# Gate weights split a job earlier, the SSD state update one step later, and plain transposes in the mLSTM turn

## The chip, the cores and the metric

The kernel runs on one core of a Trainium2 chip. A core has five engines with queues of their own: TensorE (PE) multiplies matrices and transposes, VectorE (DVE), ScalarE (ACT) and GpSimd (POOL) do elementwise work, SyncE (SP) issues nearly all DMAs here. The metric is the device time of one execution in microseconds (us). Before the change three runs took 1884.36, 1888.11 and 1892.07 us; the median is 1888.11.

## The reference

A decoder layer with two parallel groups of heads over a sequence of 2048 tokens of width 1024, all in float32:

```python
h = rms_norm(x, norm_w)
proj = h @ w_in                       # 1024 x 6680
q, k, v, i, f, o, z_m, z_s, xbc, dt = split(proj)
# four mLSTM heads, chunks of 128 tokens: matrix memory C, normaliser n
hm = mlstm_chunkwise(q, k, v, log_i, log_f)
hm = hm * rsqrt(mean(hm * hm) + EPS) * w * sigmoid(o) * silu(z_m)
# two SSD groups of eight heads, chunks of 128: state h
xs, B, C = split(silu(causal_conv(xbc)))
y = ssd_chunked(xs, dt, A, B, C) + d_skip * xs
y = y * silu(z_s); y = y * rsqrt(mean over group(y * y) + EPS) * w
x = x + concat(hm, y) @ w_out
return rms_norm(x, final_norm_w)
```

In `ssd_chunked` a chunk gives `y_diag` (from its own tokens), `y_off` (from the state that the chunks before left), and then `h = decay * h + B^T (weights * x)`. In the mLSTM a chunk's rows are divided by a norm per row before they are gated.

## The kernel before, in words

The projections are large matrix products in two stages (the two halves of the sequence, 1024 tokens each) and two more stages for the output projection (one per half of the mixed columns). Each product of a pair of column blocks is a Strassen-like form of seven products; each has twelve matmuls of 128x128 by 128x512 (four slices of the inner size; high times high, high times low, low times high of a float32r split). A *job* is one such pair: 26 in each of the stages 0 and 1, 8 in each of the stages 2 and 3. `strassen` (L273) yields after each product, and the main loop (L1031) interleaves job n with the first two products of job n + 1.

The right operands (`R11`, `R21`, `T2`, `T3`, `T1`, `R22`, `T4`, high and low, 1 MB each) stay in SBUF for a whole stage. In the last job of a stage each is refilled from DRAM after its last use (`refill`, L387). Those of stage 1 are made ahead of time by `next_h` (L493), which runs in the background from the end of phase h1 on: for each of four chunks it loads two blocks of tokens into `xt` (the one buffer `t`, which the convolution's `cd` and the gates' `tz` use too), normalises them (`tok_norm`), turns them on PE (`tok_turn`, L414) some calls later, and writes seven sums out, each split into `hqh` and `hql` (three buffers `hq`, L395) and stored. The line `at(3 + i * 82 // total, bgq)` spreads its calls over the steps. `next_w` (L520) does the same with the output weights in stage 1.

A *step* is one product: `step` (L1002) prepares left operands (`left`), refills, runs what is due (`tick`, `later`), what is planned (`at`), and pulls the recurrence of the phase before along (`Weave.to`). The order of PE's instructions is the order in which the program writes them; the other engines' order is chosen by the scheduler of the framework, near the program's order. Every engine works its queue in order.

The gate columns of the projection have matmuls of their own, `gates_mm` (L541): four small loads of weights into `wg`, two DVE operations that make two sums, a split into `wgs`, then 24 matmuls with R11 and R21 and 24 with R22 and T3. For stage 1 its head is called at the head of job 26, the first of that stage, and the matmuls follow at the first and the third step.

`rec_head` (L665) does one mLSTM head: `scores`, `memory`, and four steps later `turn` (L743), where PE multiplies the rows `mx` by a diagonal matrix `dgm` (identity times the row's factor, made on POOL), which turns and scales them at once. `rec_group` (L776) does one SSD group. A chunk goes through `decay` (loads `E`, subtracts on DVE, exponential on ACT), `tokens` (DVE makes `xdt`, `cbm`, `xw` and then `E` times `cbm`), `states` (PE: the old state's part L842, then the new state L852), a step later `outs` (PE L870), and `norm` and `spread` three and five steps after that. `E` has a single buffer.

Of the kernel before, what the change touches and what calls it, by code (L numbers as in the profile page):

```python
# [10 lines left out]
F32R = mybir.dt.float32r  # L11
# [6 lines left out]
P = 128  # L18
# [51 lines left out]
def hybrid_layer(ctx, tc, x, norm_w, w_in, b_igate, b_fgate, conv_w, conv_b, dt_bias,  # L70
# [422 lines left out]
    def next_h():  # L493

        for c in range(NCH):
# [3 lines left out]
            for i in range(2):  # L499
# [4 lines left out]
                tok_norm(SUP + i * TB + c * P, None, xt)  # L504
                for _ in range(4):
                    yield
# [34 lines left out]
    def gates_mm(s, R):  # L541
        wg = r2("wg", 4 * 4 * NG)
        wv = wg.rearrange("p (o k c) -> p o k c", o=4, k=4)
# [5 lines left out]
        nc.vector.tensor_scalar_mul(wv[:, 3], wv[:, 0], -1.0)  # L549
        wh = mk([P, 1024], "t", 1, "wgs", F32R) if s else mk([P, 6, P], "g3", 2, "wgs", F32R).rearrange("p a b -> p (a b)")  # L550
        hi, lo = wh[:, 0:16 * NG], wh[:, 16 * NG:32 * NG]
        nc.scalar.copy(hi, wg)
# [112 lines left out]
    def rec_head(s, h):  # L665
# [38 lines left out]
        def memory(n):  # L704
# [26 lines left out]
            nc.gpsimd.tensor_tensor(sq, sq, mhalf, op=ALU.pow)  # L731
            dg = r5("dgm")
            nc.gpsimd.tensor_scalar_mul(dg, ident, sq)
            L["m", n] = (mx, dg)

# [7 lines left out]
        def turn(n):  # L743
            b, c = seq[n]
            mx, dg = L.pop(("m", n))
            g = L.pop(("gt", n))
            ps = rc_tile()
            for i in range(2):
                nc.tensor.matmul(ps[:, i * P:(i + 1) * P], lhsT=mx[:, i * P:(i + 1) * P], rhs=dg,
                                 start=True, stop=True)  # L750
            nc.vector.tensor_mul(g, ps[:, 0:2 * P].rearrange("p (a l) -> p a l", a=2), g)
            nc.sync.dma_start(mixd[0][b * NCH + c][:, 2 * h:2 * h + 2, :], g)
# [23 lines left out]
    def rec_group(s, g):  # L776
# [30 lines left out]
        def tokens(n):  # L807
# [7 lines left out]
            for i in range(4):  # L815
                nc.tensor.transpose(xps[:, i * P:(i + 1) * P], t[:, 2 + i, :], ident)
            xdt = r2("xdt")
            nc.vector.tensor_tensor(xdt.rearrange(v3, e=HD), xps.rearrange(v3, e=HD),
                                    bc(G["sp"][:, c, ws], HD), op=ALU.mult)
            bt = r5("bt")  # L820
            nc.scalar.copy(bt, cps[:, P:2 * P])
            cbm = r5("cbm")
            nc.vector.tensor_mul(cbm, cps[:, 0:P], tri)
            xw = r2("xw")
            nc.vector.tensor_tensor(xw.rearrange(v3, e=HD), xps.rearrange(v3, e=HD),
                                    bc(G["dend"][:, c, hs], HD), op=ALU.mult)
            E = L["E", n][0]
# [3 lines left out]
        def states(n):  # L831
# [5 lines left out]
            H = S.get("H")  # L837
            y = r2("y").rearrange("p (a l) -> p a l", a=4)
            if H is not None:
                ops = rc_tile()  # L840
                for i in range(4):
                    nc.tensor.matmul(ops[:, i * P:(i + 1) * P], lhsT=H[:, i * P:(i + 1) * P],  # L842
                                     rhs=t[:, 1, :], start=True, stop=True)
                nc.vector.tensor_mul(y, ops.rearrange("p (a l) -> p a l", a=4), ea)
                for i in range(4):
                    nc.scalar.activation(ea[:, i, :], t[:, 2 + i, :], AF.Copy, scale=dcol[:, g, i:i + 1])
                nc.vector.tensor_add(y, y, ea)
            else:
                for i in range(4):
                    nc.scalar.activation(y[:, i, :], t[:, 2 + i, :], AF.Copy, scale=dcol[:, g, i:i + 1])  # L850
            sps = rc_tile()
            nc.tensor.matmul(sps, lhsT=bt, rhs=xw, start=True, stop=True)  # L852
            if H is None:
                H = S["H"] = mk([P, GW], "H", 1, "H")
                nc.vector.tensor_copy(H, sps)
            else:
                nc.gpsimd.tensor_tensor(H.rearrange(v3, e=HD), H.rearrange(v3, e=HD),
                                        bc(G["cdec"][:, c, hs], HD), op=ALU.mult)
                nc.vector.tensor_add(H, H, sps)
            L["y", n] = y  # L860

        def outs(n):
# [14 lines left out]
            nc.vector.tensor_mul(y, y, z)  # L877
            nc.scalar.activation(z, y, AF.Square)
            nc.gpsimd.tensor_add(z[:, 0:2, :], z[:, 0:2, :], z[:, 2:4, :])
# [33 lines left out]
        for n in range(len(seq)):  # L913
            states(n)
            if s == 0 and n + 1 == len(seq):
                nc.sync.dma_start(hdd[g], S["H"])
            yield
            outs(n)
# [112 lines left out]
    for n, jb in enumerate(jobs):  # L1031
        g = jb["gen"]
        if jb["new"] and "s" in jb:
            s = jb["s"]
            gm = gates_mm(s, Rs[s]) if s else gm0
            if s:
                next(gm)
                at(1, gm)
# [34 lines left out]
        if "s" in jb and (n + 1 == len(jobs) or jobs[n + 1].get("ph") != jb["ph"]):  # L1073
            nxt = [k for k in jobs[n + 1:] if k.get("ph") == jobs[n + 1].get("ph") and k["stage"] == jobs[n + 1]["stage"]]
            wv.set(rec(jb["s"], jb["ph"]), NREC[jb["ph"][0]], 7 * len(nxt) if "s" in jobs[n + 1] else 42)
            if jb["ph"] == "h1":
                bgq = next_w() if jb["s"] else next_h()
                total = 64 if jb["s"] else 68
                for i in range(total):
                    at(3 + i * 82 // total, bgq)  # L1080
        if jb["stage"] == 2 and n + 1 < len(jobs) and jobs[n + 1]["stage"] == 3:
# [29 lines left out]
```

## Time and profile before

| what | before |
|---|---|
| median of three runs | 1888.11 us |
| profiled execution | 1880.11 us, span 1878.4 us |
| PE, PE weight loads busy | 1693.1 us (90%), 1380.0 us (73%) |
| DVE, ACT, POOL busy | 1299.4 us (69%), 899.9 us (48%), 398.6 us (21%) |
| DMA | 405.33 MB, mean 216 GB/s |
| mean granted PE clock | 0.960 of full speed |

The span runs from the first to the last instruction. Busy time of an engine is the union of its instructions. PE's matmuls overlap one another, so a group's busy time is not its cost; the distance between starts is nearer to that. The idle time that stands behind a group is that of its engine just before it, with what ended it.

### The profile page before, as it was taken

The page shows a single profiled execution, that of the slowest core. Times are in us where ns is not written, and L with a number is a line of the kernel's source. Part 1 is how long each engine was busy: PE and PEld are TensorE (multiplying, and loading weights), DVE is VectorE, ACT ScalarE, POOL GpSimd, SP SyncE. Part 2 cuts the span into 40 slices and gives each one's busy share as a digit, 9 for nine tenths or more (in the row PEclk, how much of TensorE's full clock was granted, in tenths as well). Part 3 has the DMA queues.
Part 4 walks back from the last instruction along what each step waited for, and adds up shares of the span by engine and source line. Part 5 has one row for each costly group of instructions (what it writes and reads, how often), then busy time and mean ns, then how long its engine had stood idle before and what let it go on. Part 6 is the DMA issues. An engine that isn't in the chain of part 4 may idle for free.

```text
span 1878.4 us, 25378 instructions
## 1 busy us (share of the span) xinstructions
PE 1693.1 (90%) x8200; PEld 1380.0 (73%) x8200; DVE 1299.4 (69%) x2417; ACT 899.9 (48%) x1912; POOL 398.6 (21%) x597
## 2 busy tenths in 40 slices
PE   5999999899999793998999999989979878997997
PEld 4688887788788681776788878768768667776885
DVE  7677968966657782697685886565668557863775
ACT  5345644465566551343554455555556433432443
POOL 2000303223121220032121231201112134431322
PEclk8999999999999896998999999999989989998999
DMA  5355667578778699364565758888867977578553
GB/s 149 96 166 171 192 197 214 176 244 249 233 210 233 185 308 358 98 198 134 181 181 162 240 176 271 257 285 274 270 195 256 358 264 223 185 254 336 181 161 112
DMA packets 358323, 405.33 MB, mean 216 GB/s; under 512 B 30224, under 2 KB 284432, under 8 KB 352816
## 3 DMA queue, kind: packets, MB, share of 16 engines
q1 hardware_dynamic: 358192, 403.72, 66.7%
q8 instruction: 65, 1.06, 0.2%
q14 instruction: 66, 0.54, 0.1%
HBM read 251.40 MB, written 152.24 MB: 215 GB/s over the span
## 4 chain that ended last, share of the span: by engine, by line
PE 32%; DMA 22%; DVE 12%; issue 5%; ACT 4%; SPq 3%; POOL 2%; DVEq 0%; POOLq 0%; ACTq 0%
PE pj L270 26%; DMA E<-arow 4%; DMA nmi<-mrow 3%; DVE E L797 2%; DMA we<-in_w_out 2%; DVE cd L317 2%; DMA wb<-in_w_in 1%; DMA xr<-in_x 1%; PE rc L852 1%; DMA T4l<-ws1T 1%; DMA mx<-mix 1%; DVE hql L398 1%; DMA z<-gd 1%; PE rc L870 1%; DMA ws1T<-hqh 1%
## 5 line engine op out<-in xcount | busy, mean ns | idle before, releaser
L730 POOL TENSOR_SCALAR sq<-dn,sq 128x1 f32<-128x1 f32 x64 | 50.3, 785 | 663.0 <-ACT sj L728 532.2
L270 PE MATMUL pj<-R22h,S4h 128*128 128x512 f32 x272 | 118.3, 435 | 34.7 <-ACT ob L289 19.1
L270 PE MATMUL pj<-T2h,S2h 128*128 128x512 f32 x272 | 114.9, 423 | 2.3 <-ACT T2h L441 2.3
L270 PE MATMUL pj<-T1l,S1h 128*128 128x512 f32 x272 | 107.9, 397 | 8.8 <-DMA T1l<-ws1T 7.0
L270 PE MATMUL pj<-T1h,S1h 128*128 128x512 f32 x272 | 113.1, 416 | 2.5 <-ACT ob L283 2.4
L270 PE MATMUL pj<-T4h,L22h 128*128 128x512 f32 x272 | 113.3, 416 | 1.9 <-DMA T4h<-ws1T 1.9
L270 PE MATMUL pj<-R11h,L11h 128*128 128x512 f32 x272 | 113.9, 419 | 0.0
L270 PE MATMUL pj<-R21h,L12h 128*128 128x512 f32 x272 | 112.9, 415 | 0.0
L270 PE MATMUL pj<-R22l,S4h 128*128 128x512 f32 x272 | 111.6, 410 | 0.0
L270 PE MATMUL pj<-R22h,S4l 128*128 128x512 f32 x272 | 111.6, 410 | 0.0
L270 PE MATMUL pj<-T2l,S2h 128*128 128x512 f32 x272 | 108.2, 398 | 3.2 <-DMA T2l<-ws0T 1.9
L270 PE MATMUL pj<-T3h,S3h 128*128 128x512 f32 x272 | 109.7, 403 | 0.0
L270 PE MATMUL pj<-T4l,L22h 128*128 128x512 f32 x272 | 106.9, 393 | 1.9 <-DMA T4l<-ws1T 1.9
L270 PE MATMUL pj<-T2h,S2l 128*128 128x512 f32 x272 | 108.0, 397 | 0.0
L270 PE MATMUL pj<-T1h,S1l 128*128 128x512 f32 x272 | 107.6, 396 | 0.0
L270 PE MATMUL pj<-T4h,L22l 128*128 128x512 f32 x272 | 106.9, 393 | 0.0
L270 PE MATMUL pj<-R21l,L12h 128*128 128x512 f32 x272 | 106.5, 392 | 0.0
L270 PE MATMUL pj<-R21h,L12l 128*128 128x512 f32 x272 | 106.5, 391 | 0.0
L270 PE MATMUL pj<-R11h,L11l 128*128 128x512 f32 x272 | 106.3, 391 | 0.0
L270 PE MATMUL pj<-T3l,S3h 128*128 128x512 f32 x272 | 106.1, 390 | 0.2 <-DMA T3l<-ws0T 0.2
L270 PE MATMUL pj<-T3h,S3l 128*128 128x512 f32 x272 | 106.1, 390 | 0.0
L270 PE MATMUL pj<-R11l,L11h 128*128 128x512 f32 x272 | 106.1, 390 | 0.0
(331 smaller groups left out, 4681.4 us busy)
## 6 DMA issues: line engine op xcount, KB each, us to landing
wa<-in_w_in SPq DMA_DIRECT2D x52, 512.0 KB, 5.3
s<-sum SPq DMA_DIRECT2D x52, 512.0 KB, 5.5
hd<-ob SPq DMA_DIRECT2D x32, 512.0 KB, 4.2
E<-arow SPq DMA_DIRECT2D x32, 512.0 KB, 5.4
hin<-hd SPq DMA_DIRECT2D x64, 256.0 KB, 5.6
mx<-mix SPq DMA_DIRECT2D x32, 512.0 KB, 4.4
wb<-in_w_in SPq DMA_DIRECT2D x26, 512.0 KB, 4.8
sum<-ls SPq DMA_DIRECT2D x26, 512.0 KB, 3.8
```

What stands on the lines that cost most here:

```text
L270: nc.tensor.matmul(ps, lhsT=l[:, k, :], rhs=r[:, k, :], start=start and k + n == 0, stop=k == 3 and n == 2, skip_group_check=True)
L317: nc.vector.scalar_tensor_tensor(dst, raw[:, q:q + SUP], cw[:, t, q:q + 1], dst, op0=ALU.mult, op1=ALU.add)
L398: nc.vector.tensor_sub(lo, src, hi.bitcast(F32))
L730: nc.gpsimd.tensor_scalar(sq, dn, DV * EPS, sq, op0=ALU.mult, op1=ALU.add)
L797: nc.vector.tensor_scalar(E[:, r, :], E[:, r, :], G["cum"][:, c, k:k + 1], 0.0, op0=ALU.subtract, op1=ALU.min)
L852: nc.tensor.matmul(sps, lhsT=bt, rhs=xw, start=True, stop=True)
L870: nc.tensor.matmul(yps[o:o + HD, (r // 2) * P:(r // 2 + 1) * P], lhsT=xdt[:, r * HD:(r + 1) * HD], rhs=E[:, r, :], start=True, stop=True, ...
```

## The change

Five things are changed. The head of `gates_mm` for stage 1 is called at the head of job 25, one job earlier, and its three tiles are taken from the `hq` buffers. In `rec_group` the matmul L852 and the addition to H move from `states` into a new `update`, which is called a step later, ahead of `outs`; `xw` and `bt` are made first in `tokens`; the D term is written into `y` by ACT ahead of the old state's part, which is multiplied into `ea` and added; the decay of H on POOL stays in `states`. The square in `outs` moves from ACT to POOL. In `rec_head` POOL scales `mx` in place, and `turn` transposes it. `next_h` yields six times instead of four between a load and its turn, with 84 calls over 76 steps instead of 68 over 82.

```diff
@@ next_h
-                for _ in range(4):
+                for _ in range(6):
                     yield
@@ gates_mm
-        wg = r2("wg", 4 * 4 * NG)
+        wg = mk([P, 512], "hq", 3, "wg")[:, 0:16 * NG] if s else r2("wg", 4 * 4 * NG)
...
-        wh = mk([P, 1024], "t", 1, "wgs", F32R) if s else mk([P, 6, P], "g3", 2, "wgs", F32R).rearrange("p a b -> p (a b)")
-        hi, lo = wh[:, 0:16 * NG], wh[:, 16 * NG:32 * NG]
+        if s:
+            hi, lo = (mk([P, 512], "hq", 3, "wgs", F32R)[:, 0:16 * NG] for _ in range(2))
+        else:
+            wh = mk([P, 6, P], "g3", 2, "wgs", F32R).rearrange("p a b -> p (a b)")
+            hi, lo = wh[:, 0:16 * NG], wh[:, 16 * NG:32 * NG]
@@ rec_head, memory and turn
-            dg = r5("dgm")
-            nc.gpsimd.tensor_scalar_mul(dg, ident, sq)
-            L["m", n] = (mx, dg)
+            nc.gpsimd.tensor_scalar_mul(mx, mx, sq)
+            L["m", n] = mx
...
-                nc.tensor.matmul(ps[:, i * P:(i + 1) * P], lhsT=mx[:, i * P:(i + 1) * P], rhs=dg,
-                                 start=True, stop=True)
+                nc.tensor.transpose(ps[:, i * P:(i + 1) * P], mx[:, i * P:(i + 1) * P], ident)
@@ rec_group, tokens: order now bt, xw, xdt, cbm, E times cbm
+            bt = r5("bt")
+            nc.scalar.copy(bt, cps[:, P:2 * P])
+            xw = r2("xw")
+            nc.vector.tensor_tensor(xw.rearrange(v3, e=HD), xps.rearrange(v3, e=HD),
+                                    bc(G["dend"][:, c, hs], HD), op=ALU.mult)
             xdt = r2("xdt")
...
@@ rec_group, states, update and outs
+            for i in range(4):
+                nc.scalar.activation(y[:, i, :], t[:, 2 + i, :], AF.Copy, scale=dcol[:, g, i:i + 1])
             if H is not None:
...
-                nc.vector.tensor_mul(y, ops.rearrange("p (a l) -> p a l", a=4), ea)
-                for i in range(4):
-                    nc.scalar.activation(ea[:, i, :], t[:, 2 + i, :], AF.Copy, scale=dcol[:, g, i:i + 1])
+                nc.vector.tensor_mul(ea, ops.rearrange("p (a l) -> p a l", a=4), ea)
                 nc.vector.tensor_add(y, y, ea)
...
+                nc.gpsimd.tensor_tensor(H.rearrange(v3, e=HD), H.rearrange(v3, e=HD),
+                                        bc(G["cdec"][:, c, hs], HD), op=ALU.mult)
+            L["y", n] = y
+
+        def update(n):
+            bt, xdt, xw = L["a", n]
+            H = S.get("H")
             sps = rc_tile()
             nc.tensor.matmul(sps, lhsT=bt, rhs=xw, start=True, stop=True)
...
-            nc.scalar.activation(z, y, AF.Square)
+            nc.gpsimd.tensor_mul(z, y, y)
...
             states(n)
+            yield
+            update(n)
             if s == 0 and n + 1 == len(seq):
                 nc.sync.dma_start(hdd[g], S["H"])
-            yield
             outs(n)
@@ main loop
+        if n + 1 < len(jobs) and jobs[n + 1]["new"] and "s" in jobs[n + 1]:
+            S["gm"] = gates_mm(jobs[n + 1]["s"], Rs[jobs[n + 1]["stage"]])
+            next(S["gm"])
         if jb["new"] and "s" in jb:
             s = jb["s"]
-            gm = gates_mm(s, Rs[s]) if s else gm0
+            gm = S.pop("gm") if s else gm0
             if s:
-                next(gm)
                 at(1, gm)
...
-                total = 64 if jb["s"] else 68
+                total = 64 if jb["s"] else 84
                 for i in range(total):
-                    at(3 + i * 82 // total, bgq)
+                    at(3 + i * 76 // total, bgq)
```

The new spread of 76 steps holds for `next_w` too, whose 64 calls stay.

## Rows read from the trace of the kernel before

**Rows 1.** The page's first part: busy time, share of the span and instructions of each engine.

```profile
PE 1693.1 (90%) x8200; PEld 1380.0 (73%) x8200; DVE 1299.4 (69%) x2417; ACT 899.9 (48%) x1912; POOL 398.6 (21%) x597
```

**Rows 2.** Waits of PE over the whole span: line that waited, what it waited for, us in total, times, longest.

```profile
PE rc L562 <- ACT wgs L552: 30.6, 1, 30.6
PE rc L852 <- DVE xw L825: 22.3, 14, 4.3
...
PE rc L419 <- ACT xt L412: 9.7, 1, 9.7
```

**Rows 3.** The same view of the stretch from 1100 to 1480 us.

```profile
PE pj L270 <- ACT ob L289: 13.4, 6, 4.8
```

**Rows 4.** One window of 50 us: length, busy time of each engine with its instructions, granted PE clock, DMA share, GB/s.

```profile
700.00:750.00 50.00, 17.73 (x70) 11.65 (x70) 11.63 (x26) 8.93 (x15) 1.65 (x7) 0.67 0.98 357
```

**Rows 5.** Timeline of PE: start us, length us, line, operation; in brackets the idle time before it and what ended it.

```profile
713.55 0.68 PE L749 MATMUL rc<-dgm,mx 128*128 128x128 f32 x4 [1.00 <-issue]
744.81 0.62 PE L562 MATMUL rc<-R11h,wgs 128*24 128x512 f32 x1 [30.58 <-ACT wgs L552]
...
758.49 0.40 PE L562 MATMUL rc<-R22h,wgs 128*24 128x512 f32 x1
```

**Rows 6.** Timeline of SP's DMA issues: start us, time of the issuing, line, DMA.

```profile
713.71 0.44 SPq L390 DMA_DIRECT2D T1l<-hsT  x1
...
725.07 0.42 SPq L390 DMA_DIRECT2D T4l<-hsT  x1
...
735.32 5.68 SPq L546 DMA_DIRECT2D wg<-in_w_in  x4
```

**Rows 7.** The chain of work that ended last, 655 to 800 us, in order of time: start us, us, what.

```profile
718.97 11.63 DMA R22l<-hsR
...
738.75 5.07 DMA wg<-in_w_in
...
770.19 0.22 PE rc L812 x2
...
770.52 0.44 PE rc L816 x4
770.96 2.75 PE pj L270 x12
773.71 0.86 PE rc L852 x2
```

**Rows 8.** Timeline of DVE ahead of the long wait's end, columns as in rows 5.

```profile
718.42 0.69 DVE L192 TENSOR_TENSOR L11l<-wa,L11h 128x512 fp32r<-128x512 f32 x1 [1.63 <-ACT L11h L191]
```

**Rows 9.** Groups of PE's instructions by line and form: count, busy us, mean ns, idle us before them and what ended it.

```profile
L749 PE MATMUL rc<-dgm,mx 128*128 128x128 f32 x256 | 39.0, 275 | 2.0 <-issue 2.0
...
L852 PE MATMUL rc<-xw,bt 128*128 128x512 f32 x64 | 37.0, 661 | 28.1 <-DVE xw L825 22.3 <-ACT oa L327 2.0 <-ACT ob L289 1.7
```

**Rows 10.** The three longest waits ahead of L852 in PE's timeline, columns as in rows 5.

```profile
871.71 2.05 PE L852 MATMUL rc<-xw,bt 128*128 128x512 f32 x2 [4.28 <-DVE xw L825]
...
1597.24 2.04 PE L852 MATMUL rc<-xw,bt 128*128 128x512 f32 x2 [3.93 <-DVE xw L825]
...
1652.82 1.10 PE L852 MATMUL rc<-xw,bt 128*128 128x512 f32 x2 [2.79 <-DVE xw L825]
```

**Rows 11.** Timeline of DVE and POOL around the first of them, columns as in rows 5.

```profile
865.94 1.07 DVE L797 TENSOR_SCALAR E<-E,cum 128x128 f32<-128x128 f32 x5 [0.82 <-DMA E<-arow]
...
867.51 1.29 POOL L857 TENSOR_TENSOR H<-H,cdec 128x512 f32<-128x512 f32 x1 [5.52 <-PE rc L842]
867.82 1.95 DVE L797 TENSOR_SCALAR E<-E,cum 128x128 f32<-128x128 f32 x3
...
872.36 1.22 DVE L828 TENSOR_TENSOR E<-E,cbm 128x1024 f32<-128x1024 f32 x1
```

**Rows 12.** Groups of ACT, POOL and DVE by line and form, columns as in rows 9.

```profile
L846 ACT ACTIVATE ea<-gin,dcol 128x128 f32<-128x128 f32 x120 | 38.5, 391 | 51.6 <-DVE y L844 32.7 <-issue 18.2 <-DVE mp L637 0.5
...
L192 DVE TENSOR_TENSOR L12l<-wa,L12h 128x512 fp32r<-128x512 f32 x52 | 35.7, 686 | 8.3 <-ACT L12h L191 8.1
...
L857 POOL TENSOR_TENSOR H<-H,cdec 128x512 f32<-128x512 f32 x30 | 35.7, 1189 | 96.6 <-PE rc L842 96.6
...
L192 DVE TENSOR_TENSOR L12l<-mx,L12h 128x512 fp32r<-128x512 f32 x16 | 18.6, 1160 | 0.5 <-ACT L12h L191 0.5
```

**Rows 13.** The instructions of line L733: ns shortest/median/longest, first and last start.

```profile
L733 POOL TENSOR_SCALAR dgm<-ident,sq x64: 612/688/4307, 182.2 to 1477.3; 128x128 f32<-128x128 f32 x64
```

**Rows 14.** Timeline of PE, two token turns of `next_h` (the first and the last), columns as in rows 5.

```profile
397.80 1.03 PE L419 MATMUL rc<-ident,xt 128*128 128x128 f32 x8
...
634.86 1.97 PE L419 MATMUL rc<-ident,xt 128*128 128x128 f32 x8 [9.73 <-ACT xt L412]
```

**Rows 15.** DMA issues of the stores of `next_h` (`hs`) and of `next_w`'s second half (`ws1`): count, KB each, median us from issue to landing.

```profile
hsT<-hqh SPq DMA_DIRECT2D x16, 256.0 KB, 2.8
hsT<-hql SPq DMA_DIRECT2D x16, 256.0 KB, 4.0
...
ws1T<-hqh SPq DMA_DIRECT2D x16, 256.0 KB, 5.4
...
hsR<-hqh SPq DMA_DIRECT2D x12, 256.0 KB, 3.0
hsR<-hql SPq DMA_DIRECT2D x12, 256.0 KB, 6.4
```

## The prediction before the run

> **What bounds the kernel now.** I read the page's engine totals first. TensorE (PE) is busy 90% of the span, VectorE (DVE) 69%, GpSimd (POOL) 21% [rows 1]. So PE's in-order list of matmuls sets the end, and a change is worth what it takes out of that list or out of the waits in it. The second view is therefore the list of PE's waits. One stands out: 30.6 us, once, for the gate weights `wgs`. Next come 22.3 us in 14 waits for `xw`, ahead of the SSD state matmul L852, and one wait of 9.7 us for `xt`, the token turn of the second half [rows 2]. From 1100 to 1480 us PE also waits 13.4 us, in six waits, for ScalarE (ACT) to empty a product's bank [rows 3].
>
> The next view is the windows of 50 us. In the one from 700 to 750 PE is busy 17.73 of 50 us while the DMA engines are busy 98% of it [rows 4]: the long wait lies where the first half's right operands are replaced by the second half's, and there DMA is the scarce thing. The PE timeline gives its edges: the last turn matmuls start at 713.55, the first gate matmul at 744.81, the second group of them (R22) at 758.49 [rows 5]. The SyncE (SP) queue shows why: the four loads of the gate weights are issued from 735.32 on, behind the refills, T1l at 713.71 and T4l at 725.07 among them [rows 6]. The chain of waits follows the same path: R22l lands at 718.97 + 11.63 = 730.60, the last piece of the gate weights at 738.75 + 5.07 = 743.82 [rows 7].
>
> **The change part by part.**
>
> *Gate weights early.* Loads and split of the second half move from the head of job 26 to the head of job 25, seven products ahead. Their buffers are the three `hq` ones, which the background work `next_h` must have left by then: its 84 calls are spread over 76 steps, so the last falls 6 steps ahead of job 25's head. I take it that `wgs` is there when PE is done with the turn, at 713.55 + 0.68 = 714.2 [rows 5]. What is late next? PE goes through 24 gate matmuls. They have a product's 512 columns, and twelve of those take 2.75 us [rows 7], so 5.5. Then follow the T3 product and job 27's R11 product, 2.75 us each; R11's left operand was split by 718.42 + 0.69 = 719.1 [rows 8], so that one doesn't wait. That makes 714.2 + 5.5 + 5.5 = 725.2. Then the second gate group needs R22l, which landed at 730.60. The four small loads cost SP 5.68 us of issuing [rows 6], now ahead of the refills; at worst all of it is added, 736.3. I take 733, the middle. The group then starts 758.49 − 733 = 25.5 us earlier, with bounds of 27.9 and 22.2. What follows lands meanwhile: T4l, issued at 725.07, lands at 736.7 if it takes R22l's 11.63 us, and PE wants it at about 747 (733, 5.5 of gates, three products).
>
> A new wait lies on DVE and ACT: the adds and the copy of the gate weights now stand in their queues amid job 25's splits. If DVE reaches them as the loads are issued, it stands for a landing, 5.07 us [rows 7], with the splits behind it and PE's next left operand behind those. At most two landings, 10 us, at least nothing; I take 2.
>
> *SSD state update a step later.* `states` no longer holds the matmul L852; `update` runs it a step later, ahead of `outs`, and `xw` is made ahead of `xdt` and `cbm`. All of L852's idle time is 28.1 us [rows 9]. It doesn't go entirely: DVE next makes `E` times `cbm` for L870, which PE reaches a product and a state pair later. In the worst case, a wait of 4.28 us, PE stood from 867.43 to 871.71 [rows 10], and that `E` was done at 872.36 + 1.22 = 873.58 [rows 11]. Without the wait PE is at L870 after a product (2.75) and a state pair (0.86) [rows 7], at 871.04; 2.5 us of the 4.28 remain. So 1.8 us of each wait is covered. The three longest (4.28, 3.93, 2.79 [rows 10]) keep 2.5 + 2.1 + 1.0 = 5.6. I count 28.1 − 5.6 = 22 us; bounds 28 (nothing left) and 11 (half turns up ahead of L870, since both hang on `E`'s DMA). The state H has two steps left between `update` and its next reading. The D term written straight into `y` frees ACT from waiting on DVE, 32.7 us in all [rows 12]; ACT bounds nothing in those stretches, and I count nothing, up to 5 us gained.
>
> *Plain transposes.* A turn had 2 matmuls of fp32 in 2 passes each, 256 passes in all [rows 9]. A transpose is one pass, so 128 go. Two passes of 128 columns take PE 0.22 us in the chain, four transposes 0.44 [rows 7], so 0.11 us each, 14.1 us. The second half's 24 turns of heads 1 to 3 lie where PE also waits for ACT [rows 3]; I count those at half: 40 × 0.22 + 24 × 0.11 = 11.4 us. Bounds 14.1 and 5. On POOL the scaling of a 128x256 tile takes the place of the 128x128 diagonal. The trace has no such row; it lies between the diagonal's unhindered 612 ns [rows 13] and the 1189 ns of a 128x512 product [rows 12]; I take 1.0 us, near the larger. The turn comes four steps after `memory`, which hides it.
>
> *Square on POOL.* 32 squares of 128x512 go from ACT to POOL, each about the 1189 ns of its H product [rows 12]: 38 us on an engine that is 21% busy, between `outs` and `norm`, three steps apart. Hidden in itself. But POOL hinders DVE. While POOL's H product ran (1.29 us from 867.51), three `E` subtractions took 1.95 us, where five just before took 1.07 [rows 11]; and the split L12l of stages 2 and 3, which runs among POOL's adds, takes 1160 ns against 686 before [rows 12]. 1.95 − 3 × 0.21 = 1.3 us per operation at worst, × 32 = 42 us of DVE time, and nothing at best. PE follows DVE only in part; I take a tenth, 4 us lost.
>
> [...]
>
> *`next_h` denser.* The turn of `xt` comes 6 calls after its load, not 4: 6 × 76/84 = 5.4 steps against 4 × 82/68 = 4.8. A step is (634.86 − 9.73 − 397.80)/63 = 3.6 us [rows 14] (63 steps lie between these two turns by the plan). That is 2 us more of cover against a wait of 9.73 that hangs on when the one `t` buffer is let go; the convolutions that use it next start later. I count nothing, ±8. The sums come every 0.905 steps, 3.26 us, before every 1.206, 4.35 us. A sum takes two of three `hq` buffers, each held for a cast and a subtraction (about 1.3) and the landing of its store. These took 2.8, 4.0, 3.0 and 6.4 us, 4.0 in the mean over 56 [rows 15]. So three buffers give a sum every 2 × 5.3 / 3 = 3.5 us: 0.25 us too late, × 28 sums = 7 us that ACT and DVE stand. Half reaches PE: 3.5 lost. `next_w` gets the 76 steps too: a sum every 1.19 steps, 4.28 us, before 1.28. Its later stores land in 5.4 us [rows 15], which asks for 2 × 6.7 / 3 = 4.47: 0.19 × the 28 sums of the second half of it = 5 us, of which I count half, 2.6. Bounds of both are 0 and the case of rival C.
>
> *Sum.* 25.5 − 2 + 22 + 11.4 − 4 − 3.5 − 2.6 = 46.8 us. The profiled execution had a span of 1878.4 and a time of 1880.1 us; it becomes 1831.6 and 1833.3. The median of the three runs, 1888.1, lies 8.0 above the profiled time, so the forecast is 1888.1 − 46.8 = 1841.3, say 1841 us.
>
> **The rivals.**
>
> *A, more than the sum.* The good bounds: 27.9 + 28 + 14.1 and the 9.7 of `xt`, no loss, 80 us: 1808 us. For it: PE is also slower just after a long wait (the state pair took 2.05 us after 4.28 of waiting, 1.10 after 2.79 [rows 10]). Against: the DMA that is 98% busy isn't relieved.
>
> *B, the waits only move.* The early loads push the refills or come late themselves, so that the change doesn't do what it says, and the gate hole closes by half, 13; half of L852's wait turns up at L870, 11; shorter turns wait for ACT instead, 5. 1888 − 29 = 1859 us. For it: DMA is full in just that stretch [rows 4]. Against: R22l landed 13 us ahead of the gate weights [rows 7].
>
> *C, slower.* The `hq` buffers hold `next_h` up. If stores land in L us a sum takes 2(L + 1.3)/3, and each is late by that less 3.26. With 28 sums and PE paying all, the gain without these terms, 53 us, is eaten at 1.9 us each, which is L = 6.4. At 7 us it is 2.27 × 28 = 64, 1899 us. For it: `hsR<-hql` already takes 6.4 us [rows 15]. Against: the other three kinds take 2.8 to 4.0.
>
> *D, no change.* Each added POOL operation blocks DVE for its length and PE follows each time: 32 × 1.19 + 64 × (1.0 − 0.61) = 63 us lost if DVE is always caught, 43 at its busy share of 69%, against 51 gained without the 4 above: 1880 to 1900, 1890 in the middle. For it rows 11 and 12; against it DVE's idle time.
>
> **How the numbers follow.** Forecast 1841 (its own range 1822 to 1858, short of A and B): 0.60. A 0.12, B 0.12, C 0.08, D 0.08. A measurement of this kernel tells about 0.5%, 9 us. Faster by more: forecast, A and B, 0.84; within: D, 0.08; slower: C, 0.08. The range from 1806 to 1876 leaves out C, D and A's far end.
>
> **What would show it.** Right: PE's wait near 714 us falls below 12 us and is ended by R22's load, not by `wgs`; L852's idle time is under 5 us and L870's some 5; a turn has two passes. Wrong: the gate loads still stand behind T4l in SP's order; ACT's or DVE's waits on the stores of `hq` grow by tens of us; DVE's groups take longer in the SSD stretches.

## The result and the profile after

The changed kernel takes 1827.22 us (four runs, 1823.13 to 1834.45) against 1888.12 before: a ratio of 0.9681, 95% interval 0.9642 to 0.9721, so about 60 us faster. In a second batch of runs it took 1828.8 us against 1880.35, a ratio of 0.9725 (0.9695 to 0.9755), about 52 us faster. The forecast was 1841, the range 1806 to 1876. The profiled execution took 1829.99 us with a span of 1828.2, which is 50.2 us under the span of before; the forecast for the span was 46.8 under it.

The page's engine totals of the changed kernel:

```profile
PE 1679.5 (92%) x8072; PEld 1357.2 (74%) x8072; DVE 1308.7 (72%) x2417; ACT 880.6 (48%) x1880; POOL 450.2 (25%) x629
```

Against [rows 1], PE has 128 matmuls fewer and is 13.6 us less busy; the other 36.6 us of the span are idle time that went. POOL has 51.6 us more work, DVE 9.3 us more with the same count of instructions, ACT 19.3 less.

PE's waits of the changed kernel, in the form of [rows 2]:

```profile
PE pj L270 <- ACT ob L289: 24.6, 10, 5.9
PE pj L270 <- ACT cbt L289: 13.4, 5, 5.4
PE rc L813 <- DMA gin<-gd: 12.0, 1, 12.0
...
PE pj L270 <- ACT ca L276: 9.3, 1, 9.3
...
PE rc L901 <- POOL dg L894: 4.1, 4, 1.7
...
PE rc L889 <- POOL q L883: 2.9, 4, 1.0
...
PE rc L751 <- POOL mx L735: 2.0, 1, 2.0
...
PE rc L566 <- DMA R22l<-hsR: 1.5, 1, 1.5
```

The wait of 30.6 us for `wgs` is gone. What is left of it is 1.5 us, and R22's load ends it. The waits for `xw` are gone as a kind. `xt` isn't waited for at 635 us any more, but `ca` is, at 631 us and for nearly as long. The short waits for POOL, 1.0 us in all before, come to 9.0.

The window of 50 us of [rows 4], changed kernel:

```profile
700.00:750.00 50.00, 42.96 (x189) 28.68 (x188) 22.51 (x51) 15.54 (x31) 1.60 (x6) 0.93 1.02 368
```

PE is busy 42.96 of 50 us where it was busy 17.73; the DMA engines are as full as before (1.02 against 0.98). The transfers of this window weren't made shorter, R22l's for one: issued at 714.35, it ends PE's wait at 726.84, 12.5 us later, where it took 11.63 us before [rows 7]. PE now works while they go on, since the gate weights no longer stand behind them. The edges, in PE's timeline and in SP's (the first group of gate matmuls, then the second; T1's, R22's and T4's refill):

```profile
712.03 0.44 PE L751 MATMUL rc<-ident,mx 128*128 128x128 f32 x2 [2.04 <-POOL mx L735]
712.23 0.55 PE L565 MATMUL rc<-R11h,wgs 128*24 128x512 f32 x1
...
724.93 0.39 PE L565 MATMUL rc<-R22h,wgs 128*24 128x512 f32 x1
726.84 0.41 PE L566 MATMUL rc<-R22l,wgs 128*24 128x512 f32 x1 [1.52 <-DMA R22l<-hsR]
```

```profile
651.94 0.98 SPq L546 DMA_DIRECT2D wg<-in_w_in  x2
653.68 1.82 SPq L546 DMA_DIRECT2D wg<-in_w_in  x2
...
709.74 0.48 SPq L390 DMA_DIRECT2D T1l<-hsT  x1
...
714.35 0.43 SPq L390 DMA_DIRECT2D R22l<-hsR  x1
...
720.89 0.32 SPq L390 DMA_DIRECT2D T4l<-hsT  x1
```

The four gate loads are issued at 652 us, 58 us ahead of T1's refill, where in [rows 6] they stood behind T4's. DVE comes to the gate weights at 679 and stands for nothing there:

```profile
678.87 0.25 DVE L548 TENSOR_TENSOR wg<-wg 128x96 f32<-128x96 f32 x1
...
682.34 0.55 DVE L556 TENSOR_TENSOR wgs<-wg,wgs 128x384 fp32r<-128x384 f32 x1
```

Groups of the changed kernel that answer to [rows 9, 12, 13]: the main part of the outputs (L870 before), the new state (L852 before), the turn, POOL's scaling and decay, the square on POOL, DVE's `E` subtractions (L797 before), ACT's D term.

```profile
L872 PE MATMUL rc<-E,xdt 128*64 128x128 f32 x512 | 36.5, 286 | 9.4 <-DVE y L902 3.9 <-DVE E L829 3.4 <-DVE ea L847 1.6
L857 PE MATMUL rc<-xw,bt 128*128 128x512 f32 x64 | 34.5, 621 | 1.3 <-DVE cbm L827 1.3
L751 PE MATMUL rc<-ident,mx 128*128 128x128 f32 x128 | 24.7, 275 | 2.0 <-POOL mx L735 2.0
L735 POOL TENSOR_SCALAR mx<-mx,sq 128x256 f32<-128x256 f32 x64 | 84.3, 1318 | 24.6 <-issue 18.9
L849 POOL TENSOR_TENSOR H<-H,cdec 128x512 f32<-128x512 f32 x30 | 38.2, 1272 | 74.6 <-PE rc L845 74.6
L880 POOL TENSOR_TENSOR z<-y 128x512 f32<-128x512 f32 x32 | 36.7, 1147 | 140.5 <-DVE y L879 71.9 <-DVE dend L662 37.4 <-ACT S2h L191 7.3
L798 DVE TENSOR_SCALAR E<-E,cum 128x128 f32<-128x128 f32 x256 | 72.8, 354 | 14.3 <-DMA E<-arow 14.3
L841 ACT ACTIVATE y<-gin,dcol 128x128 f32<-128x128 f32 x128 | 42.4, 395 | 4.6 <-POOL q L883 2.3 <-PE rc L872 2.3
```

Two groups of before that aren't among the rows above, L870 and the `E` subtractions:

```profile
L870 PE MATMUL rc<-E,xdt 128*64 128x128 f32 x512 | 35.0, 279 | 0.2 <-DVE E L828 0.2
L797 DVE TENSOR_SCALAR E<-E,cum 128x128 f32<-128x128 f32 x256 | 63.7, 318 | 32.2 <-DMA E<-arow 32.0
```

L857 waits 1.3 us where L852 waited 28.1, and L872 waits 9.4 where L870 waited 0.2. The turn has 128 passes, not 256 (a pass is one matmul record of the trace). ACT's D term waits 4.6 us, not 51.6.

Where along the kernel the time went is seen by laying the two PE timelines side by side: the start of the product with R22 in job n, changed minus before (worked out from the starts of L270's R22 rows, in us).

| start of R22's product in job | 25 | 26 | 51 | 52 | 57 | 67 |
|---|---|---|---|---|---|---|
| before, from the span's start | 703.15 | 770.71 | 1474.41 | 1514.25 | 1656.51 | 1861.68 |
| changed, less before | -6.8 | -31.4 | -39.2 | -45.2 | -51.8 | -50.2 |
| f0, the changed kernel again | -8.3 | -34.2 | -42.2 | -45.6 | -53.6 | -49.7 |
| e1, gates only | -1.8 | -24.4 | -21.1 | -20.8 | -17.6 | -19.0 |
| e2, SSD only | +1.2 | +0.9 | -0.1 | +0.1 | -8.3 | -8.0 |
| e3, transposes only | -2.2 | -0.6 | +0.9 | +2.4 | +8.4 | +8.2 |
| e4, `next_h` and `next_w` only | -1.0 | -4.9 | -5.2 | -11.0 | -10.9 | -10.8 |
| f1, changed, `next_w` over 82 | -5.3 | -28.2 | -33.8 | -33.4 | -41.6 | -40.0 |

Half of the gain, 24.6 us (25.9 in the repeat f0), is made between jobs 25 and 26, in the hole, as the long wait for the gate weights is called here. Another 6.0 us (3.4 in f0) come in one job, 51 to 52, where stage 1 hands over to stage 2; the prediction had nothing there. Each line is one execution, and executions of one kernel lie some 10 us apart, so the lines of the runs alone are read for where a step lies and not for its last microsecond.

### The profile page after: what moved, and what is told of

Read it like the earlier page. It is cut to its first block, busy times and chain, and to the rows that moved or that the text cites. A ratio compares the mean times of both kernels' runs of the same rounds, so it can differ in the third digit from the quotient of the medians.

```text
span 1828.2 us, 25057 instructions
## 1 busy us (share of the span) xinstructions
PE 1679.5 (92%) x8072; PEld 1357.2 (74%) x8072; DVE 1308.7 (72%) x2417; ACT 880.6 (48%) x1880; POOL 450.2 (25%) x629
## 4 chain that ended last, share of the span: by engine, by line
PE 25%; DMA 15%; DVE 7%; issue 3%; ACT 2%; SPq 1%; POOL 1%; DVEq 0%; POOLq 0%; ACTq 0%
PE pj L270 21%; DMA E<-arow 1%; DMA we<-in_w_out 1%; DVE E L798 1%; DMA nmi<-mrow 1%; DMA mx<-mix 1%; DMA gin<-gd 1%; DMA ws1R<-hqh 1%; DMA T4l<-ws1T 1%; DMA ws0T<-hql 1%; DMA ws0R<-hqh 1%; DMA ws0T<-hqh 1%; DMA xr<-in_x 1%; DMA ws1T<-hqh 1%; PE rc L872 1%
## 5 line engine op out<-in xcount | busy, mean ns | idle before, releaser
L733 POOL TENSOR_SCALAR sq<-dn,sq 128x1 f32<-128x1 f32 x64 | 46.1, 720 | 624.9 <-ACT sj L731 477.8
L270 PE MATMUL pj<-R22h,S4h 128*128 128x512 f32 x272 | 119.7, 440 | 38.1 <-ACT ob L289 24.6
L270 PE MATMUL pj<-T2h,S2h 128*128 128x512 f32 x272 | 113.4, 417 | 11.6 <-ACT ca L276 9.3
L270 PE MATMUL pj<-T1l,S1h 128*128 128x512 f32 x272 | 107.3, 395 | 7.6 <-DMA T1l<-ws1T 7.2
L270 PE MATMUL pj<-R22l,S4h 128*128 128x512 f32 x272 | 113.1, 416 | 0.0
L270 PE MATMUL pj<-T4h,L22h 128*128 128x512 f32 x272 | 111.5, 410 | 1.4 <-DMA T4h<-ws1T 1.4
L270 PE MATMUL pj<-R11h,L11h 128*128 128x512 f32 x272 | 112.7, 414 | 0.0
L270 PE MATMUL pj<-R22h,S4l 128*128 128x512 f32 x272 | 112.7, 414 | 0.0
L270 PE MATMUL pj<-T2l,S2h 128*128 128x512 f32 x272 | 109.0, 401 | 4.0 <-DMA T2l<-hsT 3.3
L270 PE MATMUL pj<-T1h,S1h 128*128 128x512 f32 x272 | 111.0, 408 | 1.4 <-ACT cbt L283 1.4
L270 PE MATMUL pj<-R21h,L12h 128*128 128x512 f32 x272 | 110.1, 405 | 0.0
L270 PE MATMUL pj<-T3h,S3h 128*128 128x512 f32 x272 | 109.3, 402 | 0.0
L270 PE MATMUL pj<-T2h,S2l 128*128 128x512 f32 x272 | 108.6, 399 | 0.0
L270 PE MATMUL pj<-T1h,S1l 128*128 128x512 f32 x272 | 107.2, 394 | 1.3 <-DVE S1l L192 1.3
L270 PE MATMUL pj<-T4l,L22h 128*128 128x512 f32 x272 | 106.6, 392 | 1.9 <-DMA T4l<-ws1T 1.9
L270 PE MATMUL pj<-T4h,L22l 128*128 128x512 f32 x272 | 106.7, 392 | 0.0
L270 PE MATMUL pj<-R11h,L11l 128*128 128x512 f32 x272 | 106.6, 392 | 0.0
L270 PE MATMUL pj<-R11l,L11h 128*128 128x512 f32 x272 | 106.5, 391 | 0.0
L270 PE MATMUL pj<-T3h,S3l 128*128 128x512 f32 x272 | 106.3, 391 | 0.0
L270 PE MATMUL pj<-R21l,L12h 128*128 128x512 f32 x272 | 106.3, 391 | 0.0
L270 PE MATMUL pj<-R21h,L12l 128*128 128x512 f32 x272 | 106.3, 391 | 0.0
L270 PE MATMUL pj<-T3l,S3h 128*128 128x512 f32 x272 | 106.3, 391 | 0.0
```

The lines of the kernel that those rows point to most:

```text
L270: nc.tensor.matmul(ps, lhsT=l[:, k, :], rhs=r[:, k, :], start=start and k + n == 0, stop=k == 3 and n == 2, skip_group_check=True)
L733: nc.gpsimd.tensor_scalar(sq, dn, DV * EPS, sq, op0=ALU.mult, op1=ALU.add)
```

## Experiments

First each part of the change was put alone into the kernel before (e1 to e4, one batch), then single parts were taken out of the changed kernel (f1 to f3 with a repeat f0; g1 to g4). Savings in us are the ratio's distance from 1 times 1888; where two kernels of one batch are compared, the medians are subtracted. For e1 to e4 the medians of their batch (1882.83 for the kernel before) give a little less than the ratios: 21.2, 14.1, 3.0 and 13.2 us.

**e1, the gate weights alone.**

```diff
+        wg = mk([P, 512], "hq", 3, "wg")[:, 0:16 * NG] if s else r2("wg", 4 * 4 * NG)
...
+            S["gm"] = gates_mm(jobs[n + 1]["s"], Rs[jobs[n + 1]["stage"]])
+            next(S["gm"])
...
```

Expected: 

> The kernel before with the gate weights split at the head of job 25 in the hq buffers, and nothing else. Theory (the parts add up, and the hole at the change of the halves is the largest part): PE's wait for wgs goes, the second gate group (R22) starts 23 to 28 us earlier, what is left is a wait for R22l, and the time falls by 22 to 30 us. Rival (the old next_h spread, 82 steps, keeps hq too long, so the gate weights need the other spread to work): the wait for wgs stays over 10 us and the time falls by less than 15. Second rival (the refills, not the gate weights, were the bound): the hole closes by half, 13 us.

Measured: 1861.63 us, ratio 0.9868 (0.9832 to 0.9904), 25 us saved. Two rows of its waits of PE:

```profile
PE rc L855 <- DVE xw L828: 24.7, 14, 4.1
...
PE rc L566 <- DMA R22l<-hsR: 1.9, 1, 1.9
```

The gate hole closes as far as it does in the whole change, with R22's load as the next limit, and the waits for `xw` stay. The edits to the gate weights and to the SSD group don't share a gain.

**e2, the SSD part alone**, with `update`, the new order in `tokens` and the D term in `y`, and the square left on ACT.

```diff
...
+            yield
+            update(n)
...
-            yield
             outs(n)
```

Expected: 

> The kernel before with only the changes of the SSD group: update a step later, xw first, D term into y. The square stays on ACT. Theory: L852's idle time of 28 us falls under 5, L870's rises to about 5, the time falls by 18 to 25 us. Rival (both hang on E's DMA, the wait moves): the time falls by 10 us or less, and L870 waits 10 us or more.

Measured: 1868.73 us, ratio 0.9917 (0.9884 to 0.9949), 16 us saved, less than the 18 to 25 expected. Its groups of the main part and of the new state:

```profile
L871 PE MATMUL rc<-E,xdt 128*64 128x128 f32 x512 | 38.5, 297 | 8.0 <-DVE y L901 4.6 <-DVE E L828 2.9 <-DVE r L890 0.6
L856 PE MATMUL rc<-xw,bt 128*128 128x512 f32 x64 | 34.6, 622 | 1.8 <-DVE cbm L826 1.7
```

The wait ahead of the new state goes, and 8.0 us of it come back one step later ahead of L871. Only 2.9 of these wait for the `E` product that the prediction named. The larger piece waits for DVE's last operation of `spread` (L901), which reads an `rc` buffer in PSUM as L871 writes one; that the buffer is what holds L871 up is read from the code, and no run shows it.

**e3, the transposes alone.**

```diff
-            nc.gpsimd.tensor_scalar_mul(dg, ident, sq)
+            nc.gpsimd.tensor_scalar_mul(mx, mx, sq)
...
-                nc.tensor.matmul(ps[:, i * P:(i + 1) * P], lhsT=mx[:, i * P:(i + 1) * P], rhs=dg,
+                nc.tensor.transpose(ps[:, i * P:(i + 1) * P], mx[:, i * P:(i + 1) * P], ident)
```

Expected: 

> The kernel before with only the plain transposes of the mLSTM turn. Theory: 128 passes of 0.11 us go, 14.1 us of PE time, and the time falls by 8 to 14 us. Rival (PE's time in the mLSTM stretches is covered by its waits for ACT and DMA): the time falls by less than 5 us, and PE's wait for banks that ACT empties grows by what was won.

Measured over ten runs: 1879.79 us, ratio 0.998 (0.9961 to 0.9999), 0.2 to 7 us saved. The profiled execution was the longest of the ten, so the signs of its line in the table say little. A turn is shorter by what was foretold: between the products of jobs 5 and 9, where PE has no waits to speak of, PE gains 1.8 us over 8 turns, 0.23 each, and the changed kernel gains the same 1.8 there. A part of it is taken away again by a new wait of PE:

```profile
PE rc L748 <- POOL mx L732: 6.6, 4, 2.0
```

POOL's scaling takes 1416 ns in the mean here, and at four turns PE stands up to 2.0 us for it. The rival's sign was that PE's waits for banks that ACT empties (`ob`, `cbt`) grow by what was won; they are 36.9 us here and 34.6 before, so they take only a part. Where the rest stays isn't shown.

**e4, the spread of the background work alone**, six steps between load and turn, 84 calls, 76 steps for `next_h` and `next_w`.

```diff
-                for _ in range(4):
+                for _ in range(6):
...
-                total = 64 if jb["s"] else 68
+                total = 64 if jb["s"] else 84
...
-                    at(3 + i * 82 // total, bgq)
+                    at(3 + i * 76 // total, bgq)
```

Expected: 

> The kernel before with only the other spread of the background work: six steps of cover, 84 calls in 76 steps, next_w's 64 calls in 76 steps. Theory of the prediction: hq is short of buffers by 0.2 us a sum, the time rises by 3 to 9 us, with xt's wait of 9.7 us gone or moved to another place. Rival: the last turn's wait goes and nothing takes its place, the time falls by 5 to 10 us.

Measured: 1869.66 us, ratio 0.9922 (0.9885 to 0.9959), 15 us saved where a loss was forecast. Its waits of PE have this instead of the wait for `xt`:

```profile
PE pj L270 <- ACT ca L276: 9.3, 1, 9.3
```

So the wait for `xt` gave way to one for `ca` of nearly the same length. By the table, the largest single step lies between jobs 51 and 52 (-5.8 us), where not `next_h` but `next_w` runs.

The four ratios add up to 59 us and the four medians to 51.5; the whole change saved 60 us in its first measurement and 52 in its second. So nothing large is shared or lost between the parts, though with intervals of 4 to 7 us to either side of e1, e2, e3 and e4 a shared 10 us could hide. The square isn't among the four; g1 takes it alone.

**f0 to f2, how long `next_w` runs.** f0 is the changed kernel again; f1 spreads `next_w` over 82 steps as before, f2 over 70, with `next_h` at 76 in all three.

```diff
-                    at(3 + i * 76 // total, bgq)
+                    at(3 + i * (82 if jb["s"] else 76) // total, bgq)
```

Expected of f0: 

> The changed kernel itself, timed again beside the three below. Every theory expects a ratio to the kernel before of about 0.968, 60 us less.

Expected of f1: 

> The changed kernel with the calls of next_w, the output weights of stage 1, over 82 steps as before; next_h keeps its 76. Theory (what e4 won, some 13 us, comes from next_w being done 6 steps earlier, ahead of the crowded change to stage 2; in e4's profile all of it arises after job 46): the time rises by 6 to 13 us against f0. Rival (it comes from next_h): no change within 4 us. The prediction had next_w's denser calls as a loss of 2.6: then the time falls.

Expected of f2: 

> The changed kernel with the calls of next_w over 70 steps, another 6 fewer. If an earlier end of next_w is what counts, a further gain of up to 8 us; if the hq buffers then hold ACT and DVE up, as the prediction thought, a loss of 5 to 15 us and PE's waits for ACT (ob, cbt) grow.

Measured: 1828.8 (ratio 0.9725, so 52 us less than before where 60 were expected), 1837.5 (0.9772, 0.9738 to 0.9807) and 1831.02 us (0.9737, 0.9708 to 0.9766). Six steps more cost 8.7 us; six steps fewer bring nothing that can be told. SP's queue at the end of stage 1 shows what the six steps do. In f1:

```profile
1432.05 0.79 SPq L537 DMA_DIRECT2D ws1T<-hqh  x1
1437.26 0.32 SPq L537 DMA_DIRECT2D ws1T<-hql  x1
1437.63 0.42 SPq L346 DMA_DIRECT2D gd<-oa  x1
1438.10 0.44 SPq L346 DMA_DIRECT2D gd<-ob  x1
1438.64 0.84 SPq L390 DMA_DIRECT2D T2h<-ws0T  x1
```

And what SP waited for there, 1425 to 1450 us of f1:

```profile
SPq L537 <- DVE hql L398: 4.3, 1, 4.3
```

The changed kernel at the same place:

```profile
1424.74 0.43 SPq L346 DMA_DIRECT2D gd<-oa  x1
1426.86 0.32 SPq L346 DMA_DIRECT2D gd<-ob  x1
1427.27 0.40 SPq L390 DMA_DIRECT2D T2h<-ws0T  x1
```

In f1 a background store stands at the head of SP's queue until DVE has made the split that it stores; the store of the job's own results and the refills of stage 2 stand behind it. T2's refill is issued 2.0 us ahead of job 51's product with R22 (1440.59), in the changed kernel 8.0 us ahead (1435.24); in the kernel before it was 1.1 us (1473.27 against 1474.41). PE then waits for refills in f1:

```profile
PE pj L270 <- DMA T2l<-ws0T: 1.7, 1, 1.7
...
PE pj L270 <- DMA T1l<-ws0T: 1.5, 1, 1.5
```

In the changed kernel these waits come to 0.4 us. From job 51's product with R22 to job 52's it takes 40.3 us in f1 and 39.8 before, but 33.8 in the changed kernel, 34.5 in f2 and 34.1 in e4. All runs fall into these two groups: with `next_w` over 82 steps (before, e1, e2, e3, f1) PE waits 1.9 to 3.9 us for stage 2's refills and the stretch takes 39.8 to 41.3 us; with 76 or 70 steps (the other nine) it waits 0 to 0.6 and takes 33.8 to 36.4. Of the 6.5 us between f1 and the changed kernel here, 2.8 are waits for refills, 2.0 are a wait for POOL's `mx` and 1.2 a longer wait for `gin`; that the last two come from the same cause isn't shown. The last background store lies at 1405 us in the changed kernel and at 1383 in f2: both are clear of the handover, so f2 has nothing more to win. The rest of the 8.7 us fits a second place, 1340 to 1440 us, where PE waits 8.5 us for ACT to empty a convolution's product (`cbt`, L289) in f1, 2.8 in the changed kernel and 3.4 in f0. The table's line of f1 can't settle it: at job 26, before `next_w` begins, f1 is already 3.3 to 6.1 us behind the two executions of the changed kernel.

**f3, the changed kernel with the old turn** (the e3 edit reversed).

Expected: 

> The changed kernel with the diagonal matmuls of the mLSTM turn put back. Theory (PE's saving of 0.22 us a turn counts only where PE is bound, the rest is taken up by waits for ACT and DMA, as in e3): the time rises by 3 to 6 us against f0. Rival (the saving counts in full once the other waits are gone): it rises by 10 to 14 us. Second rival (POOL's scaling, 1318 ns, hinders more than PE's passes cost): it falls.

Measured: 1841.56 us, ratio 0.9788 (0.9751 to 0.9825), 12.8 us more than f0. Engine totals of f3:

```profile
PE 1694.1 (92%) x8200; PEld 1375.1 (75%) x8200; DVE 1306.9 (71%) x2417; ACT 880.6 (48%) x1880; POOL 421.0 (23%) x629
```

PE has 128 passes and 14.6 us more than in the changed kernel, and by the medians nearly all of it reaches the end. Here the transposes are worth 13, in e3 some 4 (0.2 to 7); the intervals overlap a little, so that the worth grows once the other waits are gone is likely and not shown.

**g1, the changed kernel with the square back on ACT.**

```diff
-            nc.gpsimd.tensor_mul(z, y, y)
+            nc.scalar.activation(z, y, AF.Square)
```

Expected: 

> The changed kernel with the square of outs back on ScalarE. The prediction charged the square on POOL with 4 us by its hindering DVE, bounds 0 and 42: then the time falls by 4 us against f0, and L901's and L889's waits for POOL (some 7 us in all) go. Rival (ACT is what PE waits for, and 20 us less on ACT help): the time rises by 3 to 8 us. Third: no change within 3 us.

Measured: 1834.12 us, ratio 0.9732 (0.9707 to 0.9757), which can't be told from the changed kernel: its time lies 5 us above f0's, in another batch, and its ratio 0.0007 above. Its row of `E` subtractions:

```profile
L798 DVE TENSOR_SCALAR E<-E,cum 128x128 f32<-128x128 f32 x256 | 65.4, 325 | 12.4 <-DMA E<-arow 12.4
```

With the squares on POOL one takes 354 ns, without them 325: 7.4 us of DVE over 256, as against the 36.7 us that the squares take on POOL. The difference holds in every run: 342 to 354 ns in the seven kernels with the squares on POOL, 309 to 331 in the seven with them on ACT. By the start and end times of the changed kernel, the 171 subtractions with nothing on POOL beside them take 280 ns in the mean and the 17 beside H's decay alone 637; only 10 of the 256 overlap a square. The squares cost the kernel nothing that can be measured. The waits for POOL's `q` and `dg` don't go with the squares either: 2.6 and 4.6 us in this run.

**g2, the changed kernel with the old SSD code**, the square on ACT with it (the e2 edit and g1's, reversed).

Expected: 

> The changed kernel with the SSD group as before (update inside states, square on ACT). Theory (as e2 alone, with the waits of E's DMA partly taking the place of xw's): the time rises by 13 to 18 us against f0. Rival (as with the transposes, more counts when the other waits are gone): it rises by 20 to 26 us, near the 22 of the prediction less its 4 for POOL.

Measured: 1847.63 us, ratio 0.9799 (0.9773 to 0.9825). Its waits of PE have the old kind again:

```profile
PE rc L853 <- DVE xw L826: 23.5, 15, 4.0
```

Against g1, which has the new SSD code and the same square, that is 13.5 us; e2 gave 16 (14 by the medians). Both are under the 22 forecast.

**g3, `next_h` spread over 68 steps** in the changed kernel (84 calls), so that its sums end 8 steps earlier.

```diff
-                    at(3 + i * 76 // total, bgq)
+                    at(3 + i * (76 if jb["s"] else 68) // total, bgq)
```

Expected: 

> The changed kernel with next_h's 84 calls over 68 steps instead of 76. The last xt is then turned ahead of the convolutions of job 21, so the 9.3 us that PE waits near 631 us for ca (its buffer waits for cd, which waits for the one t buffer that xt holds) should go: the time falls by 5 to 9 us. Rival (prediction's rival C, the hq buffers: a sum every 2.9 us against 3.5 that three buffers give): ACT's and DVE's waits for hs stores grow and the time rises by 5 us or more.

Measured: 1823.82 us (1822.32 to 1825.24), ratio 0.9673 (0.965 to 0.9695). From 600 to 680 us PE's waits are these and no more:

```profile
PE pj L270 <- ACT cbt L289: 1.1, 1, 1.1
PE rc L751 <- POOL mx L735: 0.5, 1, 0.5
```

The wait of 9.3 us for `ca` is gone, and the product of job 25 starts 7.1 us earlier than in the changed kernel (-13.9 against -6.8 by the reckoning of the table), which it keeps to the end (-56.9 against -50.2). It has the lowest median of all. Its ratio's interval overlaps those of the changed kernel (0.9681 and 0.9725), so about 5 us of gain are likely, and the lost wait is what is shown.

**g4, `norm` and `spread` four and seven steps behind `outs`** instead of three and five, in the changed kernel.

```diff
-            later(3, lambda n=n: norm(n))
-            later(5, lambda n=n: spread(n))
+            later(4, lambda n=n: norm(n))
+            later(7, lambda n=n: spread(n))
```

Expected: 

> The changed kernel with norm and spread four and seven steps after outs instead of three and five. PE's waits for POOL at L889 and L901 (7 us in all in the changed kernel's profile) should go and the time fall by 3 to 7 us. Rival (the y buffers of the seven r2 are then short): the time doesn't fall, and DVE or ACT wait for r2.

Measured: 1825.98 us, ratio 0.9696 (0.967 to 0.9722), not to be told from the changed kernel. Two of its waits of PE:

```profile
PE rc L872 <- DVE E L829: 6.4, 8, 1.3
...
PE rc L845 <- DVE r L891: 4.9, 3, 2.1
```

The waits for POOL's `q` and `dg` (7.0 us in the changed kernel) and for `y` ahead of L872 are no longer there, and these two stand in their place. So the waits went as expected and the time didn't follow. A run with g3 and g4 together wasn't made.

## Why the prediction was right, and where not

**Gate weights: right.** 25.5 less 2 was forecast; the hole gave 24.6 us in the changed kernel (job 25 to job 26), and e1 saved 25 us as a time (21 by the medians). What was to be seen was seen: the wait near 714 us fell to 1.5 us and is ended by R22's load. In the reckoning R22's group was put at 733. Its first matmul starts at 724.93, its second, behind the wait for R22l, at 726.84; everything is 6.8 us earlier by then, so these are 731.7 and 733.6. The 2 us for DVE and ACT standing behind the gate weights didn't come, since the loads were issued 27 us ahead of their use and not next to it. Not counted was the wait for T2's refill just ahead, 0.7 us before and 3.3 now; why it grew isn't shown.

**SSD state: mechanism right, size too large.** The step that was mis-sized is "I count 28.1 − 5.6 = 22 us". The 13.5 to 16 us of g2 and e2 lie within the bounds of 28 and 11. L872 still waits 9.4 us, not 5.6, and 3.4 of it for `E`. The prediction followed one input of that matmul, `E`. In the shortened stretch other things came late too: the `rc` buffer that `spread` reads, and POOL's `q` and `dg`, 7.0 us together where `q` alone made PE wait 1.0 before. They aren't the squares' doing: g1 and e2, with the squares on ACT, each have 7.2 us of these waits for `q` and `dg`. They are what is late next once the 28 us ahead of the new state are gone.

**Transposes: right in company.** 0.23 us per turn was measured in jobs 5 to 9, where 0.22 was forecast. 11.4 us in all was forecast; f3 gives 12.8, but alone in the kernel before (e3) the transposes gave 0.2 to 7, so the sum's term is borne out only beside the other changes. The scaling on POOL takes 1318 ns, not 1.0 us, and is hidden but for one wait of 2.0 us (two, 4.1 us, in f0; four, 6.6 us, in e3).

**Square on POOL: the hindrance is real, the loss isn't seen.** 4 us were counted lost; g1 shows none, though the scatter of two batches, some 7 us, would hide a loss of that size. One of the prediction's signs of being wrong, that DVE's groups take longer in the SSD stretches, did appear, and without the loss. The 325 against 354 ns agree that DVE is hindered, as the 280 against 637 ns beside H's decay do (changed kernel, under g1); the 7.4 us of DVE against 36.7 of squares are a fifth of what rival D took for them if DVE is always caught. The bound of 42 us of DVE time supposed that each of the 32 squares delays a subtraction by 1.3 us at worst; only ten subtractions meet a square at all.

**Background spread: the wrong step.** "3.5 lost" for `next_h` and "2.6" for `next_w` had together the wrong sign: e4 saves 15 us. The prediction asked only what denser sums cost at the `hq` buffers, and no cost is seen: DVE's waits, from 380 to 680 us, for the first T stores were 9.2 us before and are 2.9 now, although these stores land in 4.1 us and not 2.8. In g3, denser still, they are 5.9 us and the time doesn't rise. It didn't ask when the work ends. Ending six steps earlier takes the stores off SP's queue before stage 2's refills come, which goes with 3.4 to 6.0 us less in job 51; f1's median puts the whole worth of `next_w`'s earlier end at 8.7. The last stores and the refills go through one queue, SP's, and the prediction looked at that queue for the gate loads alone. No run takes `next_h`'s own spread out by itself, so its term is not shown; by these numbers it would be the rest of e4's 13 to 15 us, a gain and not a loss. The nothing counted for `xt` was right by the wait that took its place, `ca` with 9.3 us, and g3 shows that this one could be had as well.

**The rivals.** B fell with the hole (1.5 us left, not 13), though of its second leg, 11 us of wait turning up at L870, 9.4 did turn up at L872; C fell with the stores' waits, D with g1. A had its share of truth, since there was more to gain than the sum, but not where A looked: `next_w` isn't in it.

So the sum was 3.4 us short by the span and 14 by the medians (5 by those of the second batch), and that it came so near is partly luck, with errors of both signs: SSD 6 to 8 us too high, the losses of 2 and 4 us for standing and for the square not seen, and the spread, forecast to cost 6, gained 9 (f1, `next_w` alone) to 15 (e4). What remains open is why e1's line in the table gives back 5 us between jobs 26 and 67. It may be the scatter between executions: f0 and the changed kernel, which are the same, differ by 3 us at jobs 26 and 51 and by 0.5 at 67.

## What to carry to other kernels

A background job has two prices: what its pace costs while it runs (no loss was seen here), and what its last stores cost when a refill has to go out behind them on the same queue (8.7 us by f1's median); let it end some steps ahead of the handover. When a small operand makes a large wait in a stretch where DMA is full (here 30.6 us at a DMA share of 0.98), its load belongs ahead of that stretch, in any buffer that has come free by then. When an instruction is moved a step later, list all inputs and buffers of the next one and not only the latest: here two thirds of the wait that came back hung on something else.

## What the runs showed of the hardware

A wait of PE can cost more than its idle time. The first of two such waits in the changed kernel, in PE's timeline:

```profile
705.63 0.80 PE L270 MATMUL pj<-T2l,S2h 128*128 128x512 f32 x1 [3.31 <-DMA T2l<-hsT]
```

Windows of PE in the changed kernel behind the wait of 3.31 us for T2 and behind that of 2.04 us for `mx` (columns as in [rows 4]):

```profile
705.63:709.15 3.52, 3.52 (x9) 2.83 (x9) 0.80 (x1) 0.00 (x0) 0.00 (x0) 0.52 1.00 407
712.03:715.95 3.92, 3.92 (x11) 1.67 (x12) 1.90 (x4) 2.13 (x4) 0.08 (x3) 0.56 1.06 425
715.95:722.44 6.49, 6.49 (x30) 4.05 (x29) 1.02 (x2) 0.27 (x2) 0.00 (x0) 1.00 1.03 408
```

After each of these two waits the granted clock is low for a while, 0.52 and 0.56 in the mean of the first two windows, and then 1.00 (709.15 to 709.99 us, and the third window). In the second window nine gate matmuls of 512 columns start 0.41 us apart (3.72 us from 712.23 to 715.95), in the third the same kind starts every 0.23 us. So the 2.04 us of waiting cost 9 × 0.18 = 1.6 us more behind them, by an estimate from these starts. Not every wait has this price: behind the 1.52 us for R22l at 726.84 the granted clock stays at 1.00 (726.84 to 732.26 us) and the gate matmuls start 0.23 to 0.25 us apart.

The slow start may move with the wait. L857's matmuls take 621 ns in the mean where L852's took 661 [rows 9], which is 64 × 0.04 = 2.6 us less. L872's take 286 where L870's took 279, which is 512 × 0.007 = 3.6 us more (281, or 1.0 us more, in f0). The prediction's sum counted neither.
